# Five first FFN pairs at half width instead of six, conv steps over fewer weight chunks, and four smaller moves in a two-layer trunk

## The chip, the cores and the metric

The kernel runs on one core of a Trainium2 chip. The metric is the device time of one execution in microseconds (us). The names of the engines are those of the profile: PE multiplies matrices (its weight loads are listed as PEld), DVE, ACT and POOL work on tiles of 128 partitions, SP issues most of the transfers.

## The reference

Two layers over 512 tokens of width 1024, all in float32. Every norm is over the channels of a token.

```python
# layer 0
a = glu(rmsnorm(h) @ w_pw1 + b_pw1)
y = silu(layernorm(causal_depthwise_conv31(a) + b_dw))
h = h + y @ w_pw2 + b_pw2
h = h + (silu(gate) * up) @ w_down            # gate, up = split(rmsnorm(h) @ w_up)
k, v = split(rmsnorm(h) @ w_kv)               # shared by the layers behind
# layer 1
q = rmsnorm(h) @ w_q                          # 16 heads of 64, 4 key/value heads
p = softmax([q k^T / 8 + bias, sink])         # band of 128, blocks of 128 queries
h = h + (p v) @ w_o
h = h + (silu(gate) * up) @ w_down
out = rmsnorm(h)
```

The hidden width of both FFNs is 2816, that is 11 pairs of 128 columns.

## The kernel before

**Data.** `h` lies transposed: 8 tiles of 128 channels x 512 tokens. A product runs with a weight block as the fixed operand and tokens on the free axis, 512 at a time ("full width") or 256 ("half width").

**Weights.** A list of chunks (`PLAN`), each 128x1024 float32 or 512 KB, is worked off in one fixed order. `get` hands out the next chunk. It loads ahead on SP (`load`), and three chunks ahead it splits: ACT casts the high part (L203), DVE subtracts it for the low part (L204). A product (`mm3`) is then three matmuls: high weight by high input (L262), high by low (L263), low by high (L264). A chunk is 24 such matmuls. A few chunks are used unsplit (L260).

**Order in time.** A first stage does the norm, the first pointwise product and the convolution for the first 256 tokens (h0). Then comes the stage that this change is about. For the first half of the tokens, PE runs the second pointwise product (`pw2`) and the first 6 pairs of the FFN (`HALVES0[0]`), at half width. Beside it, in `background`, the other engines finish the convolution of the second 256 tokens (h1): ACT multiplies a tap (L603, the first of a tile L601), POOL adds the tap's product (L604) and at a tile's end adds the sum of its taps to that of DVE (L615), DVE does the rest of the taps (L611). Then PE does `pw2` and the same 6 pairs for the second half of the tokens, and from there on everything is at full width: 5 pairs, keys and values, the queries, attention with the output projection, the FFN of layer 1.

**Pacing.** `job` gives a background generator points (chunk, steps): by that chunk so many steps shall have been recorded, and `pace` runs them when a chunk is fetched. h1 has 20 steps in its first 8 chunks and the rest by the 42nd. After the last pair of channel tiles come its squares (`squares`, L640), one step later its sums (`sums`, L649), then the scales. A scheduler then sets the final order on each engine.

**The norm between them.** `Next` collects a norm while the input for the next product is made: ACT scales `h` for the high part (L382), DVE subtracts for the low part (L383), ACT squares (L336), and `Rms.add` sums the 8 squares with 7 adds (L340) on POOL. `step1` sums over the channels on PE (L350), turns it into a scale on DVE (L352) and POOL (L354) and spreads it through ACT (L362) and PE (L375).

**Buffers that matter.** The tap products `pr` have 8 buffers: an L603 writes into one only when POOL is done with it. Behind L603 on ACT stand the casts L203, and behind those the splits L204 on DVE.

**Attention.** A `unit` is four heads by 128 queries: scores on PE (L927), bias and minimum on DVE (L930), exponential on ACT (L937), a reciprocal on DVE (L939), the scaling on POOL (L941), transposes on PE (L948), their split on ACT and DVE (L951, L952), the product with the values on PE (L262 to L264 with operands `pth`, `ptl`, `vq`), and its split. `pipeline` runs 8 units for each half of the heads, one stage later each step, in between the matmuls of a projection (`on_step`). What is left over after the projection's last matmul is run by `drain`.

**The end.** `Fin` does the last two pairs' second product by halves of the tokens, fa and fb, and their norm. fb squares on ACT (L1047), adds the first squares on POOL (L1049), sums on PE (L1035), computes the scale (L1066, L1068, L1070), spreads it on PE (L1080) and copies the spread on ACT (L1082); POOL scales `n_pool` tiles from that copy (L1089), DVE the others from the bank of the spread (L1095).

Of the kernel before, what the change touches and what calls it, by code (L numbers as in the profile page):

```python
# [10 lines left out]
F32 = mybir.dt.float32  # L11
# [6 lines left out]
P = 128  # L18
# [3 lines left out]
KT = D // P  # L22
FT = FF // P
TAPS = 31
# [4 lines left out]
BAND = 2 * P  # L29
# [1 line left out]
EPS = 1e-6  # L31
NEG = -1e30
N_WARM = 7
HALVES0 = ((0, 6), (6, 11))
HALVES1 = ((0, 6), (6, 9))
LAST = (9, 11)
N_POOL = ((13, 13, 12, 12), (17, 15, 15, 15))
# [112 lines left out]
def hybrid_trunk(ctx: ExitStack, tc: tile.TileContext, xT, W, prm_in, wdw_in, sinks, relb, onehot, outT):  # L150
    nc = tc.nc
# [20 lines left out]
    def temp():  # L172
        return tmp.tile([P, 512], F32, tag="tmp", name=uid("tmp"))
# [35 lines left out]
    def job(gen, *points):  # L209

        jobs.append([gen, points, 0])
# [30 lines left out]
    due = [0.0]  # L242
# [34 lines left out]
    ALL = slice(0, S)  # L277
    HALF = (slice(0, 256), slice(256, 512))
# [31 lines left out]
    ones_m = cpool.tile([P, P], F32, tag="ones_m", name="ones_m")  # L310
# [14 lines left out]


    class Rms:
        def __init__(self, bc, tok=ALL):
            self.acc = None
            self.bc, self.tok, self.w = bc, tok, tok.stop - tok.start  # L330
            self.eng = nc.gpsimd
            self.stage = 0

        def add(self, t):
# [168 lines left out]
        return hid  # L503

    class Next:
        def __init__(self, gains, x=None, bc=None, tok=ALL):
            self.gains, self.tok = gains, tok
            self.x, self.rms = x, None
            self.bc = bc

        def on_h(self, i):
            if self.x is None:
                self.x = {self.gains[0]: Act(KT)}
            if self.rms is None:
                self.bc = new_bc() if self.bc is None else self.bc
                self.rms = Rms(self.bc, self.tok)
            g = self.gains[0]
            split_scaled(cut(self.x[g][i], self.tok), h[i][:, self.tok], col(g, i))
            self.rms.add(h[i][:, self.tok])
# [28 lines left out]
    with tc.tile_pool(name="conv", bufs=2) as cv:  # L548
# [29 lines left out]
        class Half:  # L578
            def __init__(self, hf, after=()):
                self.hf, self.after, self.last = hf, after, ()  # L580
                self.y = quads.tile([P, KT, W2], F32, tag="quad", name=uid("y"))
                self.shift = None
                self.st = None
                self.n_steps = sum(TAPS - n + 1 for n in N_POOL[hf]) + KT + 7

            def taps(self, ct, c):
                n_pool = N_POOL[self.hf][ct // 2]
# [111 lines left out]
            def background(self):  # L699

                gen = self.conv()
                due = []
                for p in range(KT // 2):
                    for s in range(TAPS - N_POOL[self.hf][p] + 1):
                        next(gen)
                        while due and due[0][0] <= s:
                            due.pop(0)[1]()
                        yield
                    due = [(3, self.shift_rows)] if p == 0 else []
                    due += [(4, lambda p=p: self.squares(p)), (8, lambda p=p: self.sums(p))]  # L710
                for _, f in due:
                    f()
                    yield
                self.scales_a()
                yield
                self.scales_b()
                yield
                yield
                yield
                self.spread()  # L720
                yield from self.rows(True)
# [98 lines left out]
            late.gate()  # L820
        h1.after = [h0.silu]
        base = seen[0]
        job(second, (base, 0), (base + 8, 20), (base + 42, h1.n_steps - early))
        x0 = {"ffn0": Act(KT)}
        bc0 = new_bc()
        n0 = Next(("ffn0",), x0, bc0, HALF[0])
        pw2(h0.z, n0)
        ffn_part(0, 0, x0["ffn0"], HALF[0], n0.rms)
        flush()
# [28 lines left out]
    if True:  # L858
# [52 lines left out]
        def unit(gp, jp, n):  # L911
# [3 lines left out]
            w = nk * P  # L915
            rows = [slice(HD * g, HD * (g + 1)) for g in range(2)]
            heads = [gp * 8 + g * 4 + 2 * jp + e for g in range(2) for e in range(2)]
            sc = at.tile([P, 4, 1 + BAND], F32, tag="sc", name=uid("sc"))
            sinks4 = sk.rearrange("p (a g j e) -> p a g j e", a=2, g=2, j=2)[:, gp, :, jp, :]
            nc.gpsimd.tensor_copy(sc[:, :, 0].rearrange("p (g e) -> p g e", g=2), sinks4)  # L920
            m4 = small.tile([P, 4], F32, tag="m4", name=uid("m4"))
# [18 lines left out]
            for j in range(4):  # L940
                nc.gpsimd.tensor_scalar(sc[:, j, 1:1 + w], sc[:, j, 1:1 + w], sm[:, j:j + 1], 0.0,  # L941
                                        op0=ALU.mult, op1=ALU.add)
            yield
            pts = []
            for kb_ in range(nk):
# [24 lines left out]
        def pipeline(gp):  # L970
            units = [unit(gp, jp, n) for n in range(NBLK) for jp in range(2)]
            done = 0
            for t in range(len(units) + 3):
                for d in (3, 2, 1, 0):
                    if 0 <= t - d < len(units):
                        next(units[t - d])
                yield

        def drain(it):
# [36 lines left out]
    class Fin:  # L1016
        def __init__(self, hf):
            self.hf, self.tok = hf, HALF[hf]
            self.banks, self.hg = [bank() for _ in range(4)], []
            self.n_pool = 2 + hf  # L1020

        def down(self, kp, g):
            whi, wlo = get("down", 1, kp, g)
# [13 lines left out]

        def rows(self, g, other=lambda n, ins: None):

            n_add = 4 if self.hf else KT  # L1040
            for i in range(g * 4, g * 4 + 4):
                t = h[i][:, self.tok]
                add = nc.vector.tensor_add(t, self.banks[i // 2][:, (i % 2) * 256:(i % 2) * 256 + 256], t)
                if i == KT - 1:
                    other(2, add.ins)
                sq = res.tile([P, 256], F32, tag="sq", name=uid("sq"), bufs=5)
                nc.scalar.square(sq, t)  # L1047
# [30 lines left out]
        def spread(self):  # L1078
            self.pb = bank()[:, 0:256]
            nc.tensor.matmul(self.pb, ones_m, self.diag, start=True, stop=True)  # L1080
            self.bc = temp()[:, 0:256]
            nc.scalar.copy(self.bc, self.pb)  # L1082

        def store(self, i, t, q=nc.sync):
            q.dma_start(outT[i][:, self.tok], t)
# [29 lines left out]
    for n, (kp, g) in enumerate(steps):  # L1115
        fb.down(kp, g)
        if n == 1:
            fa.sums()
        elif n == 2:
            fb.rows(0)  # L1120
            fa.spread()
        elif n == 3:
            fb.rows(1, fill)
    fa.out_pool()
    fb.sums(fill)
    fb.spread()
# [29 lines left out]
```

## Time and profile before

| | us |
|---|---|
| three runs | 1122.11, 1123.65, 1123.83 |
| their median | 1123.65 |
| the profiled execution, its own time | 1122.53 |
| its span in the profile | 1120.7 |
| PE busy in it | 1103.7 |
| DVE busy | 663.5 |
| ACT busy | 509.2 |
| POOL busy | 324.0 |

A row of the timeline gives start, duration, engine, line, operation, output and inputs, and the number of instructions that it joins; in square brackets stands the idle time just before them and what ended it. A row of a window gives its bounds and length, then for PE, PEld, DVE, ACT and POOL the busy time and the number of instructions, then the granted PE clock (1.00 is full speed), the share of the DMA engines and GB/s. A matmul's duration in the timeline is longer than the distance to the next, because matmuls overlap.

### The profile page before, as it was taken

What the parts mean: (1) busy time and instruction counts of PE and PEld (TensorE: products, weight loads), DVE (VectorE), ACT (ScalarE), POOL (GpSimd) and SP (SyncE); (2) the same over time, 40 slices, a digit from 0 to 9 for tenths busy, and PEclk for the clock granted to TensorE, in tenths of its full rate; (3) what the DMA queues carried; (4) which work ended last, traced back from release to release, by engine and by line L of the source; (5) the groups of instructions that cost most, each with busy time, mean ns of one, the idle gap of its engine ahead of it and who ended that gap; (6) DMA issues with size and microseconds to landing.
All of it is one profiled execution on the core that took longest, in us unless ns stands there. A gap on an engine that the chain in (4) does not pass through costs nothing.

```text
span 1120.7 us, 16124 instructions
## 1 busy us (share of the span) xinstructions
PE 1103.7 (98%) x6140; PEld 963.7 (86%) x6140; DVE 663.5 (59%) x1072; ACT 509.2 (45%) x898; POOL 324.0 (29%) x425
## 2 busy tenths in 40 slices
PE   9999998999999999999999999999999999999997
PEld 8888888999999998888888777888888888888886
DVE  4999996977756544533575585674443433444455
ACT  3887787746544322323343564553332211232233
POOL 3999699810200001211230232241111100110014
PEclk9999999999999999999999999999999999999998
DMA  9227054585555542233232111123323232333322
GB/s 357 103 31 83 28 179 133 166 266 177 182 180 181 185 151 95 93 113 94 94 94 93 59 38 39 38 76 98 100 87 110 94 94 94 99 103 100 94 94 76
DMA packets 41722, 128.16 MB, mean 114 GB/s; under 512 B 4491, under 2 KB 12844, under 8 KB 41644
## 3 DMA queue, kind: packets, MB, share of 16 engines
q1 hardware_dynamic: 40924, 126.56, 36.4%
q8 instruction: 48, 0.79, 0.3%
q10 hardware_dynamic: 720, 0.57, 0.2%
q14 instruction: 30, 0.25, 0.1%
HBM read 121.87 MB, written 5.24 MB: 113 GB/s over the span
## 4 chain that ended last, share of the span: by engine, by line
PE 90%; DVE 3%; ACT 3%; issue 2%; POOL 1%; DMA 1%; POOLq 0%; SPq 0%; ACTq 0%; DVEq 0%
PE bank L262 26%; PE bank L263 26%; PE bank L264 25%; PE bank L562 9%; PE bank L927 1%; PE bank L649 1%; PE bank L948 1%; ACT pr L603 1%; POOL pr L604 1%; DVE quad L383 1%; ACT whi L203 1%; DVE wlo L204 0%; DVE bank L611 0%; DVE sc L930 0%; DMA raw<-in_W_dram 0%
## 5 line engine op out<-in xcount | busy, mean ns | idle before, releaser
L263 PE MATMUL bank<-quad,whi 128*128 128x512 f32 (+1 forms) x1584 | 543.6, 343 | 1.7 <-DVE quad L383 1.7
L262 PE MATMUL bank<-quad,whi 128*128 128x512 f32 (+1 forms) x1584 | 543.8, 345 | 0.2
L264 PE MATMUL bank<-quad,wlo 128*128 128x512 f32 (+1 forms) x1584 | 542.9, 343 | 0.0
L204 DVE TENSOR_TENSOR wlo<-raw,whi 128x1024 fp32r<-128x1024 f32 x200 | 269.3, 1347 | 318.2 <-ACT whi L203 310.1
L203 ACT CAST whi<-raw 128x1024 fp32r<-128x1024 f32 x200 | 209.4, 1048 | 355.1 <-PE bank L263 301.2
L263 PEld LDWEIGHTS bank<-quad,whi 128*128 128x128 f32 x1584 | 301.0, 190 | 37.5 <-DVE quad L383 2.8
L262 PEld LDWEIGHTS bank<-quad,whi 128*128 128x128 f32 x1584 | 300.7, 190 | 36.5 <-ACT quad L966 0.6
L264 PEld LDWEIGHTS bank<-quad,wlo 128*128 128x128 f32 x1584 | 300.9, 190 | 34.5 <-DVE wlo L204 0.2
L472 POOL TENSOR_TENSOR tmp<-tmp,tmp 128x512 f32<-128x512 f32 x32 | 45.6, 1425 | 485.1 <-DVE tmp L471 471.5
L604 POOL TENSOR_TENSOR pr<-pr,pr 128x256 f32<-128x256 f32 x208 | 160.5, 822 | 11.0 <-ACT pr L603 11.0
L562 PE MATMUL bank<-quad,w 128*128 128x256 f32 x512 | 114.7, 384 | 0.7 <-DMA w<-in_W_dram 0.7
L611 DVE SCALAR_TENSOR_TENSOR bank<-apad,wdw,bank 128x256 f32<-128x256 f32 x248 | 113.2, 485 | 3.5
L562 PEld LDWEIGHTS bank<-quad,w 128*128 128x128 f32 x512 | 98.5, 193 | 14.9 <-DVE quad L537 0.9
L603 ACT ACTIVATE pr<-apad,wdw 128x256 f32<-128x256 f32 x208 | 99.6, 503 | 23.8 <-POOL pr L604 21.7
L340 POOL TENSOR_TENSOR tmp<-tmp,tmp 128x256 f32<-128x256 f32 (+1 forms) x42 | 45.2, 1076 | 135.2 <-ACT tmp L336 111.1
L470 ACT ACTIVATE tmp<-tmp 128x512 f32<-128x512 f32 x32 | 20.1, 632 | 86.5 <-DVE tmp L469 86.5
L941 POOL TENSOR_SCALAR sc<-sc,sm 128x256 f32<-128x256 f32 (+1 forms) x64 | 30.7, 500 | 86.8 <-DVE sm L939 86.7
L386 ACT CAST quad<-tmp 128x512 fp32r<-128x512 f32 (+1 forms) x48 | 27.8, 584 | 28.9 <-POOL tmp L472 25.0
L471 DVE TENSOR_TENSOR tmp<-bank,rsbc 128x512 f32<-128x512 f32 x32 | 22.1, 691 | 30.1 <-PE bank L264 30.1
L383 DVE SCALAR_TENSOR_TENSOR quad<-h,prm,quad 128x512 fp32r<-128x512 f32 (+1 forms) x40 | 39.4, 1020 | 0.5 <-ACT quad L382 0.4
L937 ACT ACTIVATE sc<-sc,m 128x257 f32<-128x257 f32 (+1 forms) x64 | 30.2, 475 | 15.0 <-DVE m L930 14.8
L387 DVE TENSOR_TENSOR quad<-tmp,quad 128x512 fp32r<-128x512 f32 (+1 forms) x48 | 31.0, 651 | 2.3 <-ACT quad L386 2.3
(137 smaller groups left out, 748.6 us busy)
## 6 DMA issues: line engine op xcount, KB each, us to landing
raw<-in_W_dram SPq DMA_DIRECT2D x208, 512.0 KB, 3.5
w<-in_W_dram SPq DMA_DIRECT2D x15, 512.0 KB, 9.7
fd<-fs SPq DMA_DIRECT2D x1, 3072.0 KB, 33.8
h<-in_xT_dram SPq DMA_DIRECT2D x8, 256.0 KB, 6.3
bias<-fd SPq DMA_DIRECT2D x8, 256.0 KB, 7.2
out_dram<-res SPq DMA_DIRECT2D x13, 128.0 KB, 1.8
w<-in_W_dram SPq DMA_DIRECT2D x2, 256.0 KB, 4.3
out_dram<-res ACTq DMA_DIRECT2D x3, 128.0 KB, 2.4
```

The costliest lines, as they stand in the source:

```text
L203: nc.scalar.copy(hi, r)
L204: lo_engine[0].tensor_sub(lo, r, f32(hi))
L262: nc.tensor.matmul(out, w[0], x[0], start=start, stop=False)
L263: nc.tensor.matmul(out, w[0], x[1], start=False, stop=False)
L264: nc.tensor.matmul(out, w[1], x[0], start=False, stop=stop)
L340: self.eng.tensor_add(sq, self.acc, sq)
L383: nc.vector.scalar_tensor_tensor(dst[1], src, g, f32(dst[0]), op0=ALU.mult, op1=ALU.subtract)
L472: nc.gpsimd.tensor_mul(t2, t1, t2)
L562: mm = nc.tensor.matmul(self.pb[:, w * W2:(w + 1) * W2], w1[ct][:, w, k, :], x[k] if x else xg[k][:, tok], start=k == 0, stop=k == KT - 1)
L603: on_act = nc.scalar.mul(pr, a[:, j:j + W2], tap(j))
L604: on_pool = nc.gpsimd.tensor_add(pr, acc, pr)
L611: on_dve = nc.vector.scalar_tensor_tensor(yt if i == nd - 1 else c, src, tap(i), c if i else self.shift, op0=ALU.mult, op1=ALU.add)
```

## The change

1. **Half width.** `HALVES0` becomes (0, 5) and (5, 11): 5 pairs at half width, twice, and 6 at full width. The plan has 202 weight loads instead of 208, since a half-width pair's 6 chunks are loaded for each half of the tokens.
2. **Conv steps.** The job for h1 ends at chunk 36 instead of 42. At its end, five steps lie between the squares and the sums of the last pair, instead of one.
3. **Norm squares.** The 7 adds L340 of the first norm in that stage (n0, 256 tokens) go from POOL to DVE.
4. **Attention.** One more step between the scaling (L941) and the transposes. The score tiles `sc` get 3 buffers instead of 2; a pipeline has 12 steps instead of 11.
5. **The end.** fb's part for POOL is 2 tiles instead of 3, so DVE has 6 instead of 5. POOL adds one square more (`n_add` 5), and one pair fewer is summed on PE. fb's spread is done twice, into two banks: ACT copies the second, DVE reads the first. fa's copy of the spread is issued after fb's last square.

```diff
-HALVES0 = ((0, 6), (6, 11))
+HALVES0 = ((0, 5), (5, 11))
...
-                self.n_steps = sum(TAPS - n + 1 for n in N_POOL[hf]) + KT + 7
+                self.n_steps = sum(TAPS - n + 1 for n in N_POOL[hf]) + KT + 11
...
-                for _, f in due:
+                for n, (_, f) in enumerate(due):
                     f()
-                    yield
+                    for _ in range(1 if n else 5):
+                        yield
...
-        job(second, (base, 0), (base + 8, 20), (base + 42, h1.n_steps - early))
+        job(second, (base, 0), (base + 8, 20), (base + 36, h1.n_steps - early))
...
-        n0 = Next(("ffn0",), x0, bc0, HALF[0])
+        n0 = Next(("ffn0",), x0, bc0, HALF[0], nc.vector)
...
-            sc = at.tile([P, 4, 1 + BAND], F32, tag="sc", name=uid("sc"))
+            sc = at.tile([P, 4, 1 + BAND], F32, tag="sc", name=uid("sc"), bufs=3)
...
                 nc.gpsimd.tensor_scalar(sc[:, j, 1:1 + w], sc[:, j, 1:1 + w], sm[:, j:j + 1], 0.0,
                                         op0=ALU.mult, op1=ALU.add)
+            yield
             yield
...
-            for t in range(len(units) + 3):
-                for d in (3, 2, 1, 0):
+            for t in range(len(units) + 4):
+                for d in (4, 3, 1, 0):
                     if 0 <= t - d < len(units):
                         next(units[t - d])
+                        if d == 1:
+                            next(units[t - d])
                 yield
...
-            self.n_pool = 2 + hf
+            self.n_pool = 2
...
-            n_add = 4 if self.hf else KT
+            n_add = 5 if self.hf else KT
...
         def spread(self):
             self.pb = bank()[:, 0:256]
             nc.tensor.matmul(self.pb, ones_m, self.diag, start=True, stop=True)
+            if self.hf:
+
+                pb = bank()[:, 0:256]
+                nc.tensor.matmul(pb, ones_m, self.diag, start=True, stop=True)
+                self.copy(pb)
+
+        def copy(self, pb):
             self.bc = temp()[:, 0:256]
-            nc.scalar.copy(self.bc, self.pb)
+            nc.scalar.copy(self.bc, pb)
...
+    with tc.issue_after(fb.squared):
+        fa.copy(fa.pb)
     fa.out_pool()
```

(`Next` and `Rms` take the engine as an argument; POOL is the default.)

In the half-width stage, on POOL, the difference of the two orders, where the second half of the norm's squares was added before (`tmp` are squares, `pr` tap products):

```order
 L604 TENSOR_TENSOR pr_1579<-pr_1557,pr_1579 128x256
-L340 TENSOR_TENSOR tmp_1606<-tmp_1477,tmp_1606 128x256
 L604 TENSOR_TENSOR pr_1583<-pr_1561,pr_1583 128x256
 L604 TENSOR_TENSOR pr_1587<-pr_1579,pr_1587 128x256
-L340 TENSOR_TENSOR tmp_1612<-tmp_1606,tmp_1612 128x256
 L604 TENSOR_TENSOR pr_1591<-pr_1583,pr_1591 128x256
 L604 TENSOR_TENSOR pr_1639<-pr_1587,pr_1639 128x256
-L340 TENSOR_TENSOR tmp_1618<-tmp_1612,tmp_1618 128x256
 L604 TENSOR_TENSOR pr_1643<-pr_1591,pr_1643 128x256
```

The adds of the squares are gone from between the adds of the tap products, whose own order is the same here.

On DVE, the difference a little earlier and at the same place (`quad_1318` is the low part of the norm's scaled input, second half of the channels; `wlo` the low part of a weight chunk):

```order
 L204 TENSOR_TENSOR wlo_1686<-raw_1529,whi_1685 128x1024
+L383 SCALAR_TENSOR_TENSOR quad_1318<-h,prm,quad_1317 128x256
+L340 TENSOR_TENSOR tmp_1606<-tmp_1477,tmp_1606 128x256
+L383 SCALAR_TENSOR_TENSOR quad_1318<-h,prm,quad_1317 128x256 x2
+L340 TENSOR_TENSOR tmp_1612<-tmp_1606,tmp_1612 128x256
+L383 SCALAR_TENSOR_TENSOR quad_1318<-h,prm,quad_1317 128x256
+L340 TENSOR_TENSOR tmp_1618<-tmp_1612,tmp_1618 128x256
+L340 TENSOR_TENSOR tmp_1624<-tmp_1618,tmp_1624 128x256
+L204 TENSOR_TENSOR wlo_1732<-raw_1573,whi_1731 128x1024
```

The adds now stand between the subtractions that make the input's low part, and the next weight split stands behind the last of them.

On PE, the end of the first attention pipeline, before: the transposes of the seventh unit (`sc_6398`), its product with the values (`pth_6521`), and the transposes of the eighth (`sc_6462`):

```order
L948 MATMUL bank_6516<-ident,sc_6398 128x128
L948 MATMUL bank_6525<-ident,sc_6398 128x128
L262 MATMUL bank_6544<-pth_6521,vq_5588 128x256
L948 MATMUL bank_6559<-ident,sc_6462 128x128 x4
L948 MATMUL bank_6568<-ident,sc_6462 128x128 x4
L263 MATMUL bank_6544<-ptl_6522,vq_5588 128x256
```

The same place now, with the seventh unit as `sc_6189` and `pth_6355`, and the sixth's product with the values as `pth_6312`, `pth_6321`:

```order
L950 MATMUL bank_6359<-ident,sc_6189 128x128
L263 MATMUL bank_6335<-ptl_6313,vq_5412 128x256
L264 MATMUL bank_6335<-pth_6312,vq_5413 128x256
L262 MATMUL bank_6335<-pth_6312,vq_5412 128x256
L263 MATMUL bank_6335<-ptl_6313,vq_5412 128x256
L264 MATMUL bank_6335<-pth_6312,vq_5413 128x256
L262 MATMUL bank_6335<-pth_6321,vq_5412 128x256
L263 MATMUL bank_6335<-ptl_6322,vq_5412 128x256
L264 MATMUL bank_6335<-pth_6321,vq_5413 128x256
L262 MATMUL bank_6335<-pth_6321,vq_5412 128x256
L263 MATMUL bank_6335<-ptl_6322,vq_5412 128x256
L264 MATMUL bank_6335<-pth_6321,vq_5413 128x256
```

Behind the last of these rows stands `L262` of `pth_6355`. Eleven matmuls of another unit have come between a unit's last transpose and the first matmul that reads it, where none stood before.

More of the change, by code (lines that the diff above doesn't have):

```diff
@@ L327, in hybrid_trunk, with __init__ @@
     class Rms:
-        def __init__(self, bc, tok=ALL):
+        def __init__(self, bc, tok=ALL, eng=nc.gpsimd):
             self.acc = None
             self.bc, self.tok, self.w = bc, tok, tok.stop - tok.start
-            self.eng = nc.gpsimd
+            self.eng = eng
             self.stage = 0
@@ L505, in hybrid_trunk, with __init__ @@
     class Next:
-        def __init__(self, gains, x=None, bc=None, tok=ALL):
-            self.gains, self.tok = gains, tok
+        def __init__(self, gains, x=None, bc=None, tok=ALL, eng=nc.gpsimd):
+            self.gains, self.tok, self.eng = gains, tok, eng
             self.x, self.rms = x, None
@@ L515, in on_h @@
                 self.bc = new_bc() if self.bc is None else self.bc
-                self.rms = Rms(self.bc, self.tok)
+                self.rms = Rms(self.bc, self.tok, self.eng)
             g = self.gains[0]
@@ L1046, in rows @@
                 sq = res.tile([P, 256], F32, tag="sq", name=uid("sq"), bufs=5)
-                nc.scalar.square(sq, t)
+                self.squared = nc.scalar.square(sq, t).ins
                 if 0 < i < n_add:
```

## The prediction

> **What bounds the kernel now.** First the page's head, busy times and slices: where is PE not busy?
>
> ```profile
> span 1120.7 us, 16124 instructions
> PE 1103.7 (98%) x6140; PEld 963.7 (86%) x6140; DVE 663.5 (59%) x1072; ACT 509.2 (45%) x898; POOL 324.0 (29%) x425
> POOL 3999699810200001211230232241111100110014
> ```
>
> PE is busy for 98%, so time comes only from fewer matmuls, from 17 us of idle time, or from matmuls that run slowly. POOL, 29% in all, is full in slices 2 to 8. PE's waits, summed by what ended them:
>
> ```profile
> PE bank L350 <- POOL tmp L340: 3.1, 1, 3.1
> PE bank L263 <- DVE quad L383: 1.7, 4, 0.9
> PE bank L263 <- DVE ptl L952: 1.3, 2, 0.7
> ```
>
> The largest stands in the half-width stage, the third in attention. The windows of both places, then two long undisturbed ones (half width, full width):
>
> ```profile
> 149.20:183.60 34.40, 30.44 (x185) 27.86 (x184) 26.04 (x38) 26.52 (x53) 34.40 (x39) 0.95 0.52 166
> 179.90:183.30 3.40, 3.40 (x18) 3.40 (x18) 1.37 (x3) 2.20 (x4) 3.40 (x5) 0.50 0.35 102
> 185.30:219.60 34.30, 34.30 (x278) 33.76 (x277) 29.73 (x43) 28.58 (x52) 34.30 (x35) 1.00 0.47 154
> 260.00:400.00 140.00, 140.00 (x1168) 139.95 (x1167) 90.27 (x103) 65.52 (x85) 6.49 (x8) 1.00 0.58 184
> 653.50:670.00 16.50, 14.53 (x107) 11.94 (x105) 12.91 (x34) 11.76 (x35) 8.09 (x16) 1.00 0.11 33
> 715.50:723.20 7.70, 6.93 (x49) 5.66 (x47) 5.81 (x16) 5.92 (x17) 3.06 (x8) 1.00 0.01 2
> 800.00:1060.00 260.00, 260.00 (x1149) 215.29 (x1148) 103.77 (x107) 68.05 (x77) 20.04 (x14) 1.00 0.31 97
> ```
>
> POOL works for all 34.40 and 34.30 us of the first and third row. In the second the clock is halved just after the wait at L350. At half width a matmul costs 140.00/1168 = 0.120 us, at full width 260.00/1149 = 0.226. So a chunk of 24 takes 2.88 us of PE at half width.
>
> **Part by part. One pair fewer at half width.** A pair is 6 chunks, 144 matmuls. Twice at half width: 288 x 0.120 = 34.5 us. Once at full width: 144 x 0.226 = 32.6. The difference is −1.9. Six casts and splits fewer lie beside PE and cost nothing. The full-width place is undisturbed, so its pace is the price.
>
> **The half-width stage.** What does POOL hold up? Rows of the timeline by engine, POOL, ACT, DVE and PE:
>
> ```profile
> 169.05 0.91 POOL L340 TENSOR_TENSOR tmp<-tmp,tmp 128x256 f32<-128x256 f32 x1
> 171.68 1.72 POOL L340 TENSOR_TENSOR tmp<-tmp,tmp 128x256 f32<-128x256 f32 x1
> 177.81 0.72 POOL L340 TENSOR_TENSOR tmp<-tmp,tmp 128x256 f32<-128x256 f32 x1
> 183.62 1.69 POOL L354 TENSOR_TENSOR rs<-ms,mhalf 128x2 f32<-128x2 f32 x1
> 227.63 2.42 POOL L615 TENSOR_TENSOR y<-y,pr 128x256 f32<-128x256 f32 x2 [8.02 <-DVE y L611]
> ```
>
> ```profile
> 181.61 0.51 ACT L603 ACTIVATE pr<-apad,wdw 128x256 f32<-128x256 f32 x1 [1.16 <-POOL pr L604]
> 182.03 1.03 ACT L203 CAST whi<-raw 128x1024 fp32r<-128x1024 f32 x1
> 185.33 0.70 ACT L362 ACTIVATE tmp<-ident,rs 128x128 f32<-128x128 f32 x2 [0.97 <-POOL rs L354]
> 185.94 1.03 ACT L203 CAST whi<-raw 128x1024 fp32r<-128x1024 f32 x1
> ```
>
> ```profile
> 167.55 3.58 DVE L383 SCALAR_TENSOR_TENSOR quad<-h,prm,quad 128x256 fp32r<-128x256 f32 x4
> 171.04 1.76 DVE L204 TENSOR_TENSOR wlo<-raw,whi 128x1024 fp32r<-128x1024 f32 x1
> 199.69 1.52 DVE L204 TENSOR_TENSOR wlo<-raw,whi 128x1024 fp32r<-128x1024 f32 x1 [0.18 <-ACT whi L203]
> ```
>
> ```profile
> 178.58 0.61 PE L350 MATMUL bank<-ones_c,tmp 128*128 128x1 f32 x4 [3.10 <-POOL tmp L340]
> 186.61 0.59 PE L375 MATMUL bank<-tmp,ones_m 128*128 128x256 f32 x2
> 201.18 0.28 PE L262 MATMUL bank<-quad,whi 128*128 128x256 f32 x1
> ```
>
> The eye goes to the wait of 3.10. With the slow 3.4 us behind it (18 matmuls where 3.4/0.120 = 28 fit, 1.2 us lost) it costs 4.3. But read on. ACT's taps wait for POOL (1.16 in the first ACT row), the casts stand behind them and come 3.9 us apart (182.03, 185.94) where PE wants one every 2.88, and the split that starts at 199.69 ends at 201.21, when PE starts on it (201.18). By then the 4.3 us of delay have been eaten: the stage goes at POOL's pace, and a PE that arrives earlier only waits earlier. So the term is not the 4.3 but how far the casts move.
>
> Seven adds at 0.72 leave POOL, 5.0 us. But the steps are denser, 36 chunks for 42. In the order as many POOL instructions as before, 38, stand ahead of L354: seven tap products have moved up into the seven places. And DVE's seven new adds (two inputs in SBUF each) press on POOL: a POOL add takes 0.91 beside L383, 1.72 beside a split, 0.72 alone. An add on DVE was timed only as other lines:
>
> ```profile
> L387 DVE TENSOR_TENSOR quad<-tmp,quad 128x256 fp32r<-128x256 f32 x8 | 3.3, 421 | 0.0
> ```
>
> With 0.42 us each, they cost POOL between 0 and 7 x 0.42 = 2.9. I take 0.25 each, as one L383 of 0.9 costs 0.19 and one split of 1.76 costs 1.0, so 1.75; with another 0.45 for splits that now fall on other adds, L354 slips by 2.2 to 185.8.
>
> The Trainium skill, page "SBUF — State Buffer", section "Who interferes with whom", says that a DVE instruction with two SBUF inputs contends with a GpSimd (POOL) instruction that reads SBUF, and that the port pair is an exclusive lock under which the later one "fully blocks". The trace agrees in kind (1.72 against 0.72). By that rule all 0.42 of each add would be lost, 2.9 and not 1.75, and the sum would be 1.1 worse; it speaks against the change.
>
> Now PE's delays. L350: the chain of squares on DVE ends earlier; from its place between the L383s I get 177.2 for 178.58, so 1.7 of the 3.1 stay. L375: it stands at place 228 of the stage instead of 210, 18 matmuls later, 68 behind L350. PE is there at 177.2 + 0.5 + 68 x 0.120 = 185.9; L354 ends at 186.7, its two L362 at 187.5; 1.6 of wait. Together 3.3 against 4.3, so PE comes 1.0 earlier to the chunk of 201.18. Its split comes later, by less than the 2.2 since DVE has no such adds behind L354: I take 0.8. So 1.8 of wait there, and 3.3 + 1.8 = 5.1 against 4.3, less 0.3 that before loses on the two chunks behind: **+0.5**. Ends: the splits don't slip and PE keeps its 1.0 and the 0.3, −1.3; the full 2.9 of slip and a halved clock behind L375 (1.2), less 0.3, +3.8. I stay near the first: only part of the adds can meet one on POOL. What covers the end of the conv is large: POOL idles 8.02 at 227.63.
>
> **Attention.** Rows of the two drains:
>
> ```profile
> 658.48 0.77 PE L948 MATMUL bank<-ident,sc 128*128 128x128 f32 x5 [0.55 <-POOL sc L941]
> 663.55 0.38 PE L263 MATMUL bank<-ptl,vq 128*128 128x256 f32 x1 [0.69 <-DVE ptl L952]
> 666.97 0.39 PE L262 MATMUL bank<-pth,vq 128*128 128x256 f32 x1 [0.57 <-ACT pth L951]
> 718.24 0.39 PE L263 MATMUL bank<-ptl,vq 128*128 128x256 f32 x1 [0.62 <-DVE ptl L952]
> ```
>
> The two windows hold 16.50 − 14.53 = 1.97 and 7.70 − 6.93 = 0.77 us of PE idle, 2.74 in all, waits for one unit's splits while nothing else is left. Now 11 matmuls of another unit (1.3 us) stand in front of such a reader, more than any of these waits. I take 2.74 less one wait of 0.55 for the scaling, which remains: **−2.2**. Ends: 0, if the softmax is late instead; −4.5, if also the restarts vanish (18 matmuls there last 0.36 to 0.39 instead of 0.28, 0.1 each, 1.8). The third `sc` buffer lets scores be written earlier. Against: the extra step lengthens the pipeline by one. What stands between the last scores and the last transposes is 5.5 us of PE work instead of 3.1, and the softmax needs
>
> ```profile
> L941 POOL TENSOR_SCALAR sc<-sc,sm 128x256 f32<-128x256 f32 (+1 forms) x64 | 30.7, 500 | 86.8 <-DVE sm L939 86.7
> L937 ACT ACTIVATE sc<-sc,m 128x257 f32<-128x257 f32 (+1 forms) x64 | 30.2, 475 | 15.0 <-DVE m L930 14.8
> ```
>
> 4 x 0.50 + 4 x 0.475 = 3.9 plus DVE's four: about 5, just covered.
>
> **The end.** Rows of the last 12 us:
>
> ```profile
> 1109.34 2.44 PE L1035 MATMUL bank<-ones_c,sq 128*128 128x1 f32 x20
> 1112.06 0.71 POOL L1068 TENSOR_TENSOR rs<-ms,mhalf 128x2 f32<-128x2 f32 x1 [0.66 <-DVE ms L1066]
> 1114.54 0.37 ACT L1082 COPY tmp<-bank 128x256 f32<-128x256 f32 x1 [0.72 <-PE bank L1080]
> 1114.94 2.05 DVE L1095 SCALAR_TENSOR_TENSOR res<-h,prm,bank 128x256 f32<-128x256 f32 x5 [0.94 <-ACT tmp L1082]
> 1114.98 2.09 POOL L1089 TENSOR_TENSOR res<-res,tmp 128x256 f32<-128x256 f32 x3 [2.22 <-ACT tmp L1082]
> ```
>
> Four sum records go, 4 x 2.44/20 = 0.5, but POOL's two tiles of fa, whose copy is later, now stand ahead of its L1068. DVE need not wait for the copy (0.4 earlier) but has six tiles at 0.41 for five. POOL has two for three, behind a second spread. **0**, between −0.5 and +0.5.
>
> **Sum.** −1.9 + 0.5 − 2.2 + 0 = −3.6. The profiled execution took 1122.53, its span and 1.8 around it; the runs' median is 1123.65, and the mean of these four executions 1123.0. From that mean: **1119.4**.
>
> **Rivals.** *The stall is the price.* If PE's 4.3 us at L350 come back whole and the splits follow: 1123.0 − 1.9 − 4.3 − 2.2 = 1114.6. For: the largest wait of the list. Against: the split that ends as PE starts on it.
>
> *POOL pays for the move.* Each L340 on DVE holds a POOL add for its whole 0.42, casts slip by 2.9, and the wait at L375 halves the clock again as the one at L350 did (0.50 in its window). Stage +3.8: 1123.0 − 1.9 + 3.8 − 2.2 = 1122.7. For: 1.72 beside a split. Against: it takes all 7 meetings and the clock. This is what the Trainium skill's page "SBUF — State Buffer" ("Who interferes with whom") would make of the move.
>
> *Attention's waits move but stay*, from the splits to the scaling: 1123.0 − 1.9 + 0.5 = 1121.6. For: about 5 us in 5.5.
>
> *The drains grow by a step*, the rival on the slower side. A drain's 16.50 us is some four steps of 4.1, and a unit's transposes and products are 8 x 0.12 + 12 x 0.117 = 2.4 of it. If a unit's chain sets the step, the added one costs 4.1 − 2.4 = 1.7 in each pipeline: 1123.0 − 1.9 + 0.5 + 3.4 = 1125.0. It decides where the softmax is later than the 5.5 us before its transposes. Against: all other steps have other work.
>
> **Numbers.** Chances: forecast 0.45 (own range 1117.5 to 1121.4), stall 0.13, POOL pays 0.22, attention stays 0.10, drains grow 0.10. The range 1115.0 to 1124.0 leaves out the last, most of the second, and little else. A measurement tells 0.2% (2.25 us) from no change: faster is below 1120.75, slower above 1125.25. Faster: 0.39 of the forecast's, 0.13, 0.05 of POOL's and 0.04 of attention's, about 0.61; slower: 0.05 of the last and 0.05 of POOL's end, 0.10; the rest 0.29.
>
> **What would show it.** Right: the wait at L350 is about half, a new one of some 1.6 stands at L375, PE reaches its fifteenth split chunk within 2 us of before, the full-width rest starts with the attention windows' waits at L952 gone. Wrong: no wait for splits behind L375 (the stall was the price); POOL adds of 1.1 and more beside L340; waits at L950 for L942 above 1 us in the drains.

## The result, and the profile after

| | before | changed | ratio, 95% interval |
|---|---|---|---|
| median of 5 runs each, us | 1123.26 (1122.11 to 1123.83) | 1116.38 (1115.55 to 1116.99) | 0.9943 [0.9931, 0.9955] |
| profiled execution, its own time | 1122.53 | 1115.77 | |
| its span | 1120.7 | 1114.0 | |

The change makes the kernel faster by 6.9 us, between 5.1 and 7.8 by the interval. The forecast was 1119.4, that is 3.6 faster. Among all runs below, one of the eleven of parts 1 and 2 alone took 6295 us, and the ratio there leaves it out.

The head of the page after, and PE's waits:

```profile
span 1114.0 us, 15803 instructions
PE 1098.9 (99%) x5994; PEld 955.7 (86%) x5994; DVE 662.3 (59%) x1074; ACT 502.6 (45%) x891; POOL 322.1 (29%) x420
```

```profile
PE bank L263 <- DVE quad L383: 3.7, 3, 1.9
PE bank L1084 <- DVE tmp L1074: 2.1, 1, 2.1
PE bank L314 <- POOL ones_m L311: 1.0, 1, 1.0
PE bank L263 <- DVE ptl L954: 0.8, 2, 0.5
PE bank L262 <- ACT quad L968: 0.5, 2, 0.3
```

The wait of 3.1 at L350 is gone. In its place L263 waits for L383 for 3.7 instead of 1.7, and the wait in the end (L1084, before L1080) has grown from 1.5 to 2.1.

PE's busy time is the smaller by 4.8 us, and its idle time by 1.9. Where in time, the starts of a few landmarks in the two traces tell. They cut the program into stretches whose matmuls are the same but for the pair and, in the last, for the sums and the second spread:

| stretch, us | before | changed | difference |
|---|---|---|---|
| start to the first L260 (start of `pw2`) | 130.3 | 129.7 | −0.6 |
| to the second half's L350 (six chunks fewer at half width) | 182.9 | 165.0 | −18.0 |
| to the L350 of the keys' and values' norm (six chunks fewer at half width, six more at full width) | 268.3 | 283.6 | +15.4 |
| to the L350 of layer 1's FFN norm (attention is in it) | 175.7 | 171.1 | −4.5 |
| to the last weight matmul | 351.6 | 351.6 | 0.0 |
| to the end | 11.9 | 12.9 | +1.0 |

The first row stands ahead of everything that the change touches; runs of unchanged code scatter there by 1.0 (129.7 to 130.7 in the fourteen traces of this study).

Six half-width chunks are 144 matmuls, 17.3 us at 0.120. So of the −18.0, −17.3 is the pair, and −0.7 the stage. With the +15.4 the pair gives −1.9, as forecast. The attention stretch gives twice what was forecast, and the end takes 1.0 longer.

**Attention.** The windows of the whole stage, before and after:

```profile
619.40:728.80 109.40, 106.60 (x672) 87.08 (x672) 71.01 (x212) 62.32 (x184) 33.03 (x78) 1.00 0.14 44
```

```profile
616.20:721.10 104.90, 103.54 (x672) 86.56 (x672) 71.00 (x212) 61.72 (x184) 33.70 (x77) 1.00 0.15 46
```

The same 672 matmuls. PE's idle time falls from 2.80 to 1.36, only 1.4 of the 4.5. The other 3.1 lie inside what the page counts as busy. The groups by line of the two stages say where (busy us and mean ns, then idle):

```profile
L927 PE MATMUL bank<-kq,quad 64*128 64x256 f32 x192 | 22.2, 297 | 0.0
L948 PE MATMUL bank<-ident,sc 128*128 128x128 f32 x112 | 17.3, 278 | 0.6 <-POOL sc L941 0.6
```

```profile
L928 PE MATMUL bank<-kq,quad 64*128 64x256 f32 x192 | 20.5, 296 | 0.0
L950 PE MATMUL bank<-ident,sc 128*128 128x128 f32 x112 | 15.4, 273 | 0.0
```

The transposes take 1.9 us less, the scores 1.7. Nothing about them has changed but their neighbours. Before, the program's order on PE changes between scores, transposes, products and weights in 108 stretches (106 counted in the trace), with pieces like two transposes, one score, one transpose; now in 97 (96 in the trace). A change of kind takes longer than none: before, a transpose followed by a score took 0.21 us to the next start on average, a transpose followed by a transpose 0.13.

**The half-width stage.** DVE and POOL after, at the place of the moved adds:

```profile
168.16 0.94 DVE L383 SCALAR_TENSOR_TENSOR quad<-h,prm,quad 128x256 fp32r<-128x256 f32 x1
169.03 0.95 DVE L340 TENSOR_TENSOR tmp<-tmp,tmp 128x256 f32<-128x256 f32 x1
169.90 1.82 DVE L383 SCALAR_TENSOR_TENSOR quad<-h,prm,quad 128x256 fp32r<-128x256 f32 x2
171.64 0.95 DVE L340 TENSOR_TENSOR tmp<-tmp,tmp 128x256 f32<-128x256 f32 x1
173.39 1.82 DVE L340 TENSOR_TENSOR tmp<-tmp,tmp 128x256 f32<-128x256 f32 x2
```

```profile
159.59 23.33 POOL L604 TENSOR_TENSOR pr<-pr,pr 128x256 f32<-128x256 f32 x23
182.88 2.41 POOL L615 TENSOR_TENSOR y<-y,pr 128x256 f32<-128x256 f32 x2
185.25 0.71 POOL L354 TENSOR_TENSOR rs<-ms,mhalf 128x2 f32<-128x2 f32 x1
```

An add of 256 elements costs DVE 0.95, not the 0.42 of L387 that I took. Since they stand between the L383s, the input's low part is late and PE waits for it, 1.88 and 0.99 us. From 170.5 on PE has half the clock again, and for 6.9 us where it was 3.4 before:

```profile
169.16 0.39 PE L263 MATMUL bank<-quad,whi 128*128 128x256 f32 x1 [1.88 <-DVE quad L383]
170.90 0.58 PE L263 MATMUL bank<-quad,whi 128*128 128x256 f32 x1 [0.99 <-DVE quad L383]
```

```profile
170.50:177.40 6.90, 6.41 (x28) 6.11 (x29) 6.80 (x8) 4.76 (x9) 6.90 (x8) 0.51 0.10 39
```

So a stall still stands in this stage, some 10 us earlier and at another line. POOL's 23 tap adds take 23.33 us, 1.01 each, where one alone took 0.72; but the 20 of the like place before, among the adds of squares, averaged 0.98. Counted from the stage's start (the first L260), L354 comes at 55.5 us, 53.3 before, and L350 at 49.5, 48.2 before.

### The profile page after: what moved, and what is told of

Read it like the earlier page. It is cut to its first block, busy times and chain, and to the rows that moved or that the text cites. A ratio compares the mean times of both kernels' runs of the same rounds, so it can differ in the third digit from the quotient of the medians.

```text
span 1114.0 us, 15803 instructions
## 1 busy us (share of the span) xinstructions
PE 1098.9 (99%) x5994; PEld 955.7 (86%) x5994; DVE 662.3 (59%) x1074; ACT 502.6 (45%) x891; POOL 322.1 (29%) x420
## 4 chain that ended last, share of the span: by engine, by line
PE 90%; DVE 5%; ACT 2%; issue 1%; POOL 1%; DMA 0%; SPq 0%; POOLq 0%; DVEq 0%; ACTq 0%
PE bank L263 26%; PE bank L262 26%; PE bank L264 26%; PE bank L562 8%; PE bank L928 1%; DVE quad L383 1%; PE bank L649 1%; ACT pr L603 1%; DVE bank L611 1%; PE bank L950 1%; DVE wlo L204 1%; DMA h<-in_xT_dram 0%; DVE sc L931 0%; PE bank L375 0%; DVE ptl L954 0%
## 5 line engine op out<-in xcount | busy, mean ns | idle before, releaser
L263 PE MATMUL bank<-quad,whi 128*128 128x512 f32 (+1 forms) x1536 | 535.2, 349 | 3.8 <-DVE quad L383 3.7
L262 PE MATMUL bank<-quad,whi 128*128 128x512 f32 (+1 forms) x1536 | 534.8, 350 | 0.5 <-ACT quad L968 0.5
L264 PE MATMUL bank<-quad,wlo 128*128 128x512 f32 (+1 forms) x1536 | 535.1, 348 | 0.0
L204 DVE TENSOR_TENSOR wlo<-raw,whi 128x1024 fp32r<-128x1024 f32 x194 | 262.5, 1354 | 322.4 <-ACT whi L203 312.3
L203 ACT CAST whi<-raw 128x1024 fp32r<-128x1024 f32 x194 | 203.3, 1049 | 360.0 <-PE bank L263 319.3
L263 PEld LDWEIGHTS bank<-quad,whi 128*128 128x128 f32 x1536 | 292.0, 190 | 40.9 <-DVE quad L383 5.0
L262 PEld LDWEIGHTS bank<-quad,whi 128*128 128x128 f32 x1536 | 291.7, 190 | 38.5 <-ACT quad L968 0.9
L264 PEld LDWEIGHTS bank<-quad,wlo 128*128 128x128 f32 x1536 | 292.1, 190 | 36.8 <-issue 0.2
L472 POOL TENSOR_TENSOR tmp<-tmp,tmp 128x512 f32<-128x512 f32 x34 | 48.4, 1425 | 486.7 <-DVE tmp L471 473.1
L611 DVE SCALAR_TENSOR_TENSOR bank<-apad,wdw,bank 128x256 f32<-128x256 f32 x248 | 113.2, 485 | 3.6
L562 PEld LDWEIGHTS bank<-quad,w 128*128 128x128 f32 x512 | 97.4, 191 | 15.4 <-DVE quad L537 1.7
L340 POOL TENSOR_TENSOR tmp<-tmp,tmp 128x256 f32<-128x256 f32 (+1 forms) x35 | 38.8, 1109 | 138.6 <-ACT tmp L336 109.1
L383 DVE SCALAR_TENSOR_TENSOR quad<-h,prm,quad 128x512 fp32r<-128x512 f32 (+1 forms) x40 | 39.5, 1020 | 0.5 <-ACT quad L382 0.4
L938 ACT ACTIVATE sc<-sc,m 128x257 f32<-128x257 f32 (+1 forms) x64 | 30.3, 476 | 15.4 <-DVE m L931 13.7
L387 DVE TENSOR_TENSOR quad<-tmp,quad 128x512 fp32r<-128x512 f32 (+1 forms) x50 | 32.8, 661 | 2.5 <-ACT quad L386 2.5
```

The costliest lines, as they stand in the source:

```text
L203: nc.scalar.copy(hi, r)
L204: lo_engine[0].tensor_sub(lo, r, f32(hi))
L262: nc.tensor.matmul(out, w[0], x[0], start=start, stop=False)
L263: nc.tensor.matmul(out, w[0], x[1], start=False, stop=False)
L264: nc.tensor.matmul(out, w[1], x[0], start=False, stop=stop)
L340: self.eng.tensor_add(sq, self.acc, sq)
```

## Experiments

All were compared with the kernel before, five rounds each.

### The attention step alone

Part 4 of the change on the kernel before:

```diff
+            sc = at.tile([P, 4, 1 + BAND], F32, tag="sc", name=uid("sc"), bufs=3)
...
+            yield
             yield
             pts = []
...
+            for t in range(len(units) + 4):
+                for d in (4, 3, 1, 0):
                     if 0 <= t - d < len(units):
                         next(units[t - d])
+                        if d == 1:
+                            next(units[t - d])
```

> Only part 4 (the third score buffer and the transposes one step later) on the kernel before. From the two traces attention (first scores to last product with the values) went from 109.3 to 104.8 us: if that is the step's own work, 1123.3 - 4.5 = 1118.8. If the step is worth only the waits that I counted (2.2) and the rest came from elsewhere, 1121.1. If the drains grow by a step, above 1124.

1118.37 us, ratio 0.9959 [0.9947, 0.9972]: −4.6. The stage takes 104.8 in its trace, as in the changed kernel. The whole 4.5 is the step's own.

### Its two halves apart

```diff
-            sc = at.tile([P, 4, 1 + BAND], F32, tag="sc", name=uid("sc"))
+            sc = at.tile([P, 4, 1 + BAND], F32, tag="sc", name=uid("sc"), bufs=3)
```

> Only the third score buffer on the kernel before, no step later. If the buffer alone lets scores run ahead, part of the 4.5 us: 1121. If it is the step that matters, no difference: 1123.3.

1122.01 us, ratio 0.9997 [0.9989, 1.0006]: nothing. The stage takes 109.3.

The other half, the extra `yield` and the pipeline over (4, 3, 1, 0), with two buffers:

> Only the later transposes on the kernel before, with two score buffers. The order has 96 changes of kind of matmul in attention, like the 97 with three buffers and unlike the 108 before; if the switches and the waits for splits are the gain, 1119 to 1120. If scores now wait for a free buffer, no gain or slower: 1123 to 1126.

1125.80 us, ratio 1.0033 [1.0019, 1.0048]: 3.7 slower, and the stage takes 115.0, though its order has as few changes (96) as the good one. The trace is of the slowest of seven runs (1124.21 to 1129.34), and 6.9 us of this stage had half the clock (654.6 to 661.5), which explains at most 3.4 of the 5.7 that it takes longer. POOL's groups in this stage, and the transposes:

```profile
L920 POOL COPY sc<-sk 128x4 f32<-128x4 f32 x14 | 3.7, 267 | 21.6 <-PE bank L949 21.6
```

```profile
L949 PE MATMUL bank<-ident,sc 128*128 128x128 f32 x112 | 17.3, 280 | 2.4 <-POOL sc L941 1.3 <-POOL sc L920 0.7 <-DVE m L930 0.2
```

L920 writes the sinks into a new score tile, the first thing a unit does. With two tiles it waits until the transposes have read an old one, and POOL's scalings stand behind it. So neither half works without the other: the step makes a tile live one step longer, and the third tile is what it then needs.

### Which wait it was

My forecast took the gain from the splits behind the transposes (L951, L952). This run takes away what stands ahead of them:

```diff
-            for j in range(4):
-                nc.gpsimd.tensor_scalar(sc[:, j, 1:1 + w], sc[:, j, 1:1 + w], sm[:, j:j + 1], 0.0,
-                                        op0=ALU.mult, op1=ALU.add)
```

> The kernel before without POOL's scaling of the probabilities (L941): this leaves the division of the softmax out. Nothing else is moved. If the transposes came late because they waited for the scaling, the gain of the attention part (4.5) comes mostly without the extra step: 1118.5 to 1120. If, as I forecast, the splits behind the transposes (L951, L952) were the wait, only the 0.6 put down to the scaling goes: 1122.2.

1117.66 us, ratio 0.9954 [0.9942, 0.9966]: −5.2, and the stage takes 104.8. That is the whole gain without the step. The transposes in it:

```profile
L945 PE MATMUL bank<-ident,sc 128*128 128x128 f32 x112 | 15.5, 272 | 0.2 <-DVE quad L964 0.2
```

They take 15.5, nearly as in the changed kernel (15.4), and the waits for the low splits (L949 here) are still 1.3. So a gain of this size comes without touching those splits, once the scaling ahead of the transposes is gone: four instructions of 0.50 on POOL, each releasing its own transpose, so that these, as I read it, trickled in between other matmuls. The profile put only 0.6 us down to it, because PE had other matmuls to fill the rest with, at the price of changing to and fro. The run takes POOL's work away as well as the wait, so how much of its gain is the one and how much the other is not told apart.

Nor do the two kernels gain in all the same places. The distances from one start to the next in the stage, added up by the kinds of the two matmuls, tell it:

| us | before | changed | without the scaling |
|---|---|---|---|
| into, between and out of transposes, without the next row | 18.5 | 14.9 | 15.4 |
| from a transpose to a product with the values | 2.2 | 0.3 | 1.6 |
| all others | 88.7 | 89.6 | 87.8 |

The larger part, 3.6, lies around the transposes, where the run without the scaling gains too. But 1.8 of the changed kernel's gain lies between a transpose and the product behind it, the place that the forecast named, and 0.9 is lost elsewhere.

### The squares alone, and undone

Part 3 on the kernel before:

```diff
+        n0 = Next(("ffn0",), x0, bc0, HALF[0], nc.vector)
```

> Only part 3 (the 7 square adds on DVE) on the kernel before, with 6 pairs and conv steps over 42 chunks. If POOL sets the pace of the half-width stage, PE's wait at L350 goes but comes back at the splits: 0 to -1.5, so 1121.8 to 1123.3. If the stall is the price, -4.3, so 1119.0. If the adds on DVE hold POOL, no gain or slower.

1122.65 us, ratio 0.9999 [0.9990, 1.0007]: nothing. Its waits:

```profile
PE bank L263 <- DVE quad L383: 3.7, 3, 1.8
PE bank L264 <- DVE wlo L204: 1.0, 1, 1.0
```

The largest wait of the kernel before (3.1) is gone, and not a tenth of a per cent has come of it: 2.0 more at L383, 1.0 at a split that before was just in time. Its trace also has 6.9 us of half clock in the stage (170.6 to 177.5) where before has 3.4. So the run swaps one stall for another; it doesn't show that a stall in this stage is free.

The reverse, the changed kernel with

```diff
-        n0 = Next(("ffn0",), x0, bc0, HALF[0], nc.vector)
+        n0 = Next(("ffn0",), x0, bc0, HALF[0])
```

> The changed kernel with the 7 square adds back on POOL. If POOL sets the pace of the stage and 7 adds of 0.7 us matter there, 2 to 4 us slower than the changed kernel: 1118.4 to 1120.4. If adds on DVE cost POOL as much as they save, no difference: 1116.4.

1117.85 us, ratio 0.9956 [0.9942, 0.9970] against 0.9943 [0.9931, 0.9955] of the changed kernel. About 1.5 slower, but the intervals overlap; it lies below what I expected.

### Fewer chunks, without and with the squares

Parts 1 and 2 on the kernel before:

```diff
+HALVES0 = ((0, 5), (5, 11))
...
+                self.n_steps = sum(TAPS - n + 1 for n in N_POOL[hf]) + KT + 11
...
+                    for _ in range(1 if n else 5):
+                        yield
...
+        job(second, (base, 0), (base + 8, 20), (base + 36, h1.n_steps - early))
```

> Only parts 1 and 2 (5 pairs at half width, conv steps over 36 chunks) on the kernel before. The pair alone gives -1.9, so 1121.4, if the stage keeps its delay. If POOL sets the pace and the denser steps fill it, the wait at L350 grows and the pair's gain is lost: 1122.5 to 1124.5.

1122.49 us, ratio 0.9996 [0.9985, 1.0007]: no difference clear of the noise, so most of the pair's 1.9 doesn't come through. The wait at L350 stands as before, and a new one at a split:

```profile
PE bank L350 <- POOL tmp L340: 3.1, 1, 3.1
PE bank L264 <- DVE wlo L204: 0.6, 1, 0.6
```

Parts 1, 2 and 3 together, that is the same lines and

```diff
+        n0 = Next(("ffn0",), x0, bc0, HALF[0], nc.vector)
```

> Parts 1, 2 and 3 on the kernel before, without the attention step and the new end. Alone, part 3 gave 0 and parts 1 and 2 gave -0.5. If they only add, 1122.2. If the adds on DVE give POOL the room that the denser conv steps need, the pair's 1.9 and some of the stall come through: 1120 to 1120.7.

1119.39 us, ratio 0.9968 [0.9957, 0.9980]: −3.6, where the parts alone gave −0.5 and −0.1. Together they give more than the sum, by 3.0 here; the run with the squares undone puts it at 1.5, within its noise. My reading, which no run isolates, is that the denser conv steps ask more of POOL, and the seven adds that leave it give the room.

The stage's length (first L260 to the second half's L350, 17.3 added where it has six chunks fewer) agrees in direction: 183.1 on average in the five traces with the stage as before (182.9 to 183.9), 183.4 with the squares alone, 183.6 and 184.0 with fewer chunks alone, 182.0 to 183.0 in the four with both. But one and the same stage scatters by 1.0, so a single trace doesn't settle it.

Much of the scatter is the clock. Four of the five traces as before have some 3.4 us of half clock in the stage and take 182.9 to 183.0; the fifth, the attention step alone, has 6.9 and takes 183.9. The shortest of all, parts 1, 2 and 3, has none. The windows of the fifth trace and of the shortest:

```profile
177.90:184.80 6.90, 6.51 (x30) 6.52 (x31) 3.71 (x4) 4.81 (x9) 6.90 (x8) 0.51 0.52 154
```

```profile
160.00:190.00 30.00, 25.73 (x197) 24.40 (x196) 28.38 (x39) 25.02 (x50) 30.00 (x31) 1.00 0.50 175
```

Compared at the same 6.9 us of half clock, five pairs take 184.0 with the adds on POOL and 182.3, 182.7 and 183.0 with them on DVE; six pairs take 183.9 and 183.4. So the move of the squares shortens the stage by 1.0 to 1.8 with five pairs and by 0.5 with six, which goes with the times, though one side of each comparison is a single trace. And a second window of half clock cost 1.0, so a stall in this stage is paid for at least in part.

### One pair further

The changed kernel with

```diff
-HALVES0 = ((0, 5), (5, 11))
+HALVES0 = ((0, 4), (4, 11))
...
-        job(second, (base, 0), (base + 8, 20), (base + 36, h1.n_steps - early))
+        job(second, (base, 0), (base + 8, 20), (base + 30, h1.n_steps - early))
```

> The changed kernel with 4 pairs at half width and conv steps over 30 chunks. Another -1.9, so 1114.5, if the conv still fits beside fewer chunks. If POOL sets the pace, its adds (105 us of conv work less what is done by then) no longer fit, PE waits for splits, and the gain is eaten: 1116 to 1119.

1118.33 us, ratio 0.9967 [0.9954, 0.9980]: 2 to 3 slower than with five pairs, although PE has 1.9 less to do. Its waits have splits and the conv's end among them:

```profile
PE bank L264 <- DVE wlo L204: 2.4, 2, 1.2
PE bank L649 <- POOL y L615: 1.2, 2, 0.7
```

The stage's own delay is 6.5 us longer than in the changed kernel (154.2 + 17.3 against 165.0). If POOL is what sets the pace, taps moved from POOL to DVE must help:

```diff
-N_POOL = ((13, 13, 12, 12), (17, 15, 15, 15))
+N_POOL = ((13, 13, 12, 12), (15, 14, 14, 14))
```

> 4 pairs at half width as in the run with 1118.3, and 2, 1, 1, 1 taps fewer on POOL and ACT for the four pairs of channel tiles of h1, more on DVE: 10 adds fewer on POOL (8 to 10 us), 10 more of 0.48 on DVE. If POOL sets the pace of the stage, the delay of 6.5 us there goes: 1112.5 to 1115. If DVE's splits are then late, 1117 to 1119.

1129.12 us, ratio 1.0057 [1.0044, 1.0071]: 10 to 11 slower than the run before it. PE's and POOL's waits:

```profile
PE bank L649 <- POOL y L615: 10.2, 2, 7.8
```

```profile
POOL y L615 <- DVE y L611: 13.8, 1, 13.8
```

POOL waits 13.8 us for DVE's taps, and PE for the conv's end. So "POOL sets the pace" is refuted as I meant it. At the conv's end DVE is the later one; the row of before showed it already (POOL idle for 8.02 at the last L615, released by L611), and I read it as cover. DVE is the late one at the end of the conv. It costs PE nothing with five pairs: POOL's wait there is 7.09 in the changed kernel, but no wait of PE at L649 stands in its list. That POOL is the late one earlier in the stage fits the runs with the squares (fewer chunks paid only when POOL was relieved), but no run shows it by itself.

### The end

The changed kernel with the end as before:

```diff
-            self.n_pool = 2
+            self.n_pool = 2 + hf
...
-            n_add = 5 if self.hf else KT
+            n_add = 4 if self.hf else KT
...
-            if self.hf:
-                pb = bank()[:, 0:256]
-                nc.tensor.matmul(pb, ones_m, self.diag, start=True, stop=True)
-                self.copy(pb)
...
-    with tc.issue_after(fb.squared):
-        fa.copy(fa.pb)
```

> The changed kernel with the end as before (part 5 undone). In the traces the stretch from fa's spread to the end is 12.8 us after and 11.8 before; if part 5 makes that, 1 us faster than the changed kernel: 1115.4. If that is chance of one execution, 1116.4.

1115.73 us, ratio 0.9937 [0.9925, 0.9950].

And on top of that the fifth square alone:

```diff
-            n_add = 4 if self.hf else KT
+            n_add = 5 if self.hf else KT
```

> The changed kernel with one spread, fa's copy where it was, 3 tiles for POOL, and only the fifth square added on POOL (4 sum records fewer). If the second spread and the late copy are what lengthened the end, 0.4 less than with the old end, 1.0 less than the changed kernel: 1115.3. If the end's length is only the landing of the last transfers, 1116.4.

1115.45 us, ratio 0.9932 [0.9920, 0.9944], the lowest of all, 0.9 below the changed kernel. The intervals of all three overlap, so the times alone don't show that the new end is worse. The fifth square moved nothing in the traces: the scale L1072 starts 3.27 us after the last weight matmul with it, 3.26 with the old end. What the new end does stands in the rows after; below them the spread with the fifth square alone.

```profile
1103.38 1.41 POOL L1100 TENSOR_TENSOR res<-res,tmp 128x256 f32<-128x256 f32 x2 [1.40 <-ACT tmp L1093]
1104.75 0.71 POOL L1072 TENSOR_TENSOR rs<-ms,mhalf 128x2 f32<-128x2 f32 x1
1105.97 1.22 PE L1084 MATMUL bank<-tmp,ones_m 128*128 128x256 f32 x2 [2.12 <-DVE tmp L1074]
1106.98 1.06 PE L1088 MATMUL bank<-tmp,ones_m 128*128 128x256 f32 x2
1107.23 2.44 DVE L1106 SCALAR_TENSOR_TENSOR res<-h,prm,bank 128x256 f32<-128x256 f32 x6 [0.53 <-PE bank L1084]
1108.08 0.37 ACT L1093 COPY tmp<-bank 128x256 f32<-128x256 f32 x1 [2.71 <-PE bank L1088]
1108.53 1.41 POOL L1100 TENSOR_TENSOR res<-res,tmp 128x256 f32<-128x256 f32 x2 [3.08 <-ACT tmp L1093]
```

```profile
1106.86 0.70 PE L1084 MATMUL bank<-tmp,ones_m 128*128 128x256 f32 x2 [1.50 <-DVE tmp L1074]
```

fa's tiles (1103.38) stand on POOL ahead of the scale (L1072), which is ready at 1104.05 and starts at 1104.75. And the second spread runs behind the first: DVE starts at 1107.23, ACT's copy of the second bank at 1108.08, and POOL's two tiles end at 1109.9. Counted from the last weight matmul, POOL ends at 8.9 here with two tiles, at 8.3 before with three, and at 7.8 in the last two runs, whose spread has the full clock. So of the +1.0 in the table, 0.6 is POOL's later end. The other 0.4 lies behind the last work, in a piece of 4.0 us here and 3.7 before; with the old end and five pairs it is 4.3, so it can't be put down to the new end, and what makes it stays open.

How much it costs depends on the clock in that moment. The spread takes 1.22 and its window has a clock of 0.50, both before and after; in the run with four pairs, which has the same new end, it has the full clock:

```profile
1110.68 0.70 PE L1084 MATMUL bank<-tmp,ones_m 128*128 128x256 f32 x2 [2.12 <-DVE tmp L1074]
1111.22 0.59 PE L1088 MATMUL bank<-tmp,ones_m 128*128 128x256 f32 x2
```

There, POOL and DVE end at 8.0 and 8.1, and last weight matmul to the end takes 12.0, against 12.9 with the slow clock; the other two traces with the new end have 12.1 and 13.0. With the old end it is 11.4 to 12.4 over nine traces, whichever the clock. So at the full clock the new end is not seen to be longer as a whole, and its work ends some 0.3 later; at half clock it is 0.6.

## Why the prediction was right, and where it was off

The direction and the range held (1115.0 to 1124.0), with 1116.4 near the low end. The working was wrong in three of its four terms.

- **One pair fewer, −1.9:** −1.9 in the trace (−17.3 and +15.4).
- **The half-width stage, +0.5:** −0.7 in this trace, −0.9 to +0.1 in the four traces with this stage. L354 slipped by the 2.2 that I forecast (55.5 us after the stage's start for 53.3). The delays of PE were wrong. The wait at L350 was to shrink to 1.7, with PE there 1.4 earlier, and another of 1.6 to appear at L375. It vanished at L350, but PE came there 1.3 later, and 3.7 stand at L383, upstream, because an L340 on DVE costs 0.95 where I priced it by 0.42, from another line. So PE is too late to wait at L375; in the trace of parts 1, 2 and 3, where no half clock follows L383, it waits 0.5 there. Right was that taking the wait at L350 away doesn't pay by itself; but I had put this down to POOL's pace, and in that run another stall took its place. And I took POOL alone for the pace: DVE sets the conv's end. What I named a reason against a gain, the same number of POOL instructions ahead of L354, is how the room was used: the tap adds took the places of the squares.
- **Attention, −2.2:** −4.5, the end that I had called an upper bound. I counted idle time in two windows, and put it down to the splits behind the transposes. That place gave 1.8. The larger part, 3.6, lies around the transposes themselves, in PE time that the page calls busy; the run without the scaling gains there too, so the scaling ahead of them, which I counted as one wait of 0.55 that stays, is the likelier cost. How much of it is the wait and how much POOL's work isn't told apart. The third buffer, which I mentioned in passing, is the condition: without it the step costs 3.7.
- **The end, 0:** +1.0 in this trace, outside of my ±0.5, with 0.6 of it in the work; I had the order of POOL right, but not that the second spread is serial with the first, nor what half a clock makes of both.

Of the rivals, *the stall is the price* falls as a forecast with the squares alone (0.9999): its 4.3 did not come back. *POOL pays for the move* falls too, by the time. The adds did hold each other up, as the Trainium skill's page "SBUF — State Buffer" ("Who interferes with whom") has it, but DVE pays as well, 0.95 for 0.42, and the move was still needed. *Attention's waits move but stay* falls with the attention step alone (−4.6). *The drains grow* did not happen; the run without the buffer is as slow as that rival, but by another way, the wait of L920 for a free score tile.

1116.4 lies below the forecast's own range (1117.5 to 1121.4); the stated range held it because it was made wide enough for the rivals. So the direction was earned, and that the time fell inside was in part luck: attention gave 2.3 more than its term and the stage 1.2 more, and the end took back 1.0.

## What to carry to other kernels

The idle time beside a wait can be less than what the wait costs: here the engine filled it with other instructions, the cost went into broken runs of one kind, and a comparison of one operation's busy time in two orders showed it. A step that rests one stage longer keeps its buffer one stage longer; give the buffer with the step, or the first instruction of the next unit will wait, with all that stands behind it on its queue. When the largest wait of a list goes and the time stays, look for the second engine that was just in time, and ask of each engine separately where in the stage it is the late one. And before two traces of a stage are compared, count the half clock in each.

## What the runs showed of the hardware

Operations that read two tiles in SBUF, on DVE and on POOL at once, took longer here: an add of 256 elements took 0.95 on DVE beside a busy POOL against the 0.42 of the like L387, and on POOL 1.72 beside a weight split against 0.72. After the wait of 3.10 at L350, PE's clock was 0.50 for 3.4 us. After waits of 1.88 and 0.99 at L383 it was 0.51 for 6.9 us in the changed kernel, while in the trace of parts 1, 2 and 3 the same two waits and a third of 0.76 left it at 1.00. The windows of half clock in this stage lasted some 3.4 us or twice that, and which of them a trace has changed with the same instructions (3.4 us in four traces, 6.9 in a fifth). The two small matmuls at the end took 1.22 and 1.06 at half clock, 0.70 and 0.59 at the full one; which of the two a run meets there varied from kernel to kernel with the same instructions.
